# A planned order of steps with new durations, and the last modulation block summed in another stage

## The chip, the core and the metric

The kernel runs on one core of a Trainium2 chip, in one launch. Its time is device microseconds (us) from the runs; a profile of one execution stands beside it, and its span is from the first to the last instruction on the core.

Engines, by the names of the profile: PE is TensorE, DVE VectorE, ACT ScalarE, POOL GpSimd, SP the engine that issues most of the DMAs. Each of them runs its instructions in the order in which the program lists them. PSUM is the memory that TensorE writes, SBUF the on-chip working memory.

## The reference

One decoder layer on 1024 tokens of 1024 channels, in float32. A conditioning row `c` gives six modulation vectors, two sub-layers follow, each with a norm ahead and a norm behind:

```python
mod = silu(c) @ w_ada + b_ada
sh1, sc1, gt1, sh2, sc2, gt2 = split(mod, 6)

h = rms_norm(x, g_pre_mix) * (1 + sc1) + sh1
proj = h @ w_in                               # 512 columns u, 3 x 512 for the gated convolution
y_a = s5_mixer(u, ...)                        # state space groups, GELU, gated linear unit
y_b = short_conv_mixer(bg, cg, v, conv_w)
y = concat(head_rms_norm(y_a, g_out_ssm, 32), head_rms_norm(y_b, g_out_conv, 8))
x = x + gt1 * rms_norm(y @ w_out, g_post_mix)

h = rms_norm(x, g_pre_ffn) * (1 + sc2) + sh2
hid = causal_dwconv(h @ w_up, ffn_conv_w)     # 2 x 2816 columns
a, v = split(hid, 2)
x = x + gt2 * rms_norm((silu(a) * v) @ w_down, g_post_ffn)
```

`gt2` is the sixth vector, number 5 in the code, and it is used in the last line only.

## The kernel before

Matmuls of float32 precision are done as three matmuls of a rounded format: each operand is split into a high part (rounded on ScalarE) and the remainder (a subtraction on VectorE or GpSimd, line 381 or 867), and `mm3` (lines 475 to 479) adds high x high, high x low and low x high. Weights come as tiles of 128x1024 in three `raw` buffers, their splits in three `hl` buffers.

The stages, in order of time: the first norm and the projection of `u`; the tables of the state space part, small and large products on GpSimd and VectorE (sites `CL`, `WB`, `Pt`); the h tiles (`t_h`, lines 714 to 725) and the projection for the convolution; the state space part; the gated linear unit (`t_glu`, `t_gate`, the product `ya`); the statistics of the heads and their scaling (`t_head_out`: a matmul that spreads the factors, VectorE's product into `yb` or `ya`, ScalarE's rounding to `yh`, GpSimd's remainder `yl`); the output projection; two norms; the up projection; the down projection, which begins after 900 us; the last norm. Up and down projections use seven products in place of eight (Strassen's scheme), whose sums and differences are made on VectorE and GpSimd. In the up projection, `t_pair_weights` loads two weight tiles per pair (22 pairs, the first two apart), makes their differences and splits, `t_up` does the matmuls, `t_combine` the sums of products, `t_gate2` the convolution taps and the gate.

The modulation vectors are made without TensorE but for one tile: a tile of 128 rows of the transposed `w_ada` is multiplied with `cbc`, the row silu(c) spread over all partitions, and summed along the row into a column of `mod` (`ada_dot`: line 631 on VectorE, line 633 on GpSimd with ScalarE's sum). Vectors 0 and 1 are made at the start. `t_ada` loads the 32 tiles of vectors 2, 4, 3 and 5 in this order, into the buffers `WB`, `WBT` and `Pt`, once the tables that had them are used. `t_ada_dot` ends each vector with its bias and, but for number 3, a product with a norm's gain; number 5 goes to column group 3 of `col`. `t_colb` then writes that column to DRAM and loads it back over `cbc`, spread over the partitions; the last norm multiplies with it (`t_half`).

The order of the work is not written out by hand. Each task is a Python generator that yields a charge ahead of each step (an engine and a duration in us), an event to wait for, or a buffer to take. `Flow.run` simulates the engines with these charges when the program is built, and the instructions are emitted in the order in which it starts them: among the steps that can start on the engine that is next, that of the lowest priority number (`PRIO`) goes first. A step with a choice of engines (`T_`, `SITES`) goes to the one that would end it first. So the charges set no time on the chip, but they set the order on every engine and queue. The charges before are

```python
    def D_(n):
        return ("run", "dve", 0.07 + 1.04e-3 * n)

    def A_(n):
        return ("run", "act", 0.094 + 0.833e-3 * n)

    def G_(n):
        return ("run", "pool", 0.15 + 2.1e-3 * n)
```

for n elements in a row; the matmuls have charges of their own at each place. Steps of the up and down projection use a helper, `E_`, with 0.155 + 1.045e-3 n for VectorE.

Of the kernel before, what the change touches and what calls it, by code (L numbers as in the profile page):

```python
# [18 lines left out]
P = 128  # L19
# [182 lines left out]
class Flow:  # L202
# [85 lines left out]
    def run(self, until=None):  # L288

        while True:  # L290
            self._settle()
            if until is not None and until.t is not None:
                return
            ready = [th for th in self.threads if th[4][0] in ("run", "load", "pick")]
            if not ready:
                break
            plan = [(self._choice(th), th) for th in ready]
            t0, e = min((c[0], c[1]) for c, _ in plan)
            (start, e, cost), th = min(
                ((c, th) for c, th in plan if c[1] == e and c[0] <= t0 + 0.02), key=lambda p: p[1][:2]  # L300
            )
            end = self._pe_end(start, cost) if e == "pe" else start + cost
            self.free[e] = end
            if th[4][0] == "load":
                th[3] = start
                th[5] = end + LAND
            else:
                th[3] = end
            th[6] = e
            self._step(th, e if th[4][0] == "pick" else None)  # L310
        assert not self.threads, [(t[0], t[1], t[4], t[2].__name__, t[3]) for t in self.threads]
# [3 lines left out]
def hybrid_layer(ctx, tc, xT, w_adaT, w_ada0, w_u, w_bcv, w_out, w_up, w_down, glu_w, vec, ssm, con, out):  # L315
# [21 lines left out]
    def nm(s):  # L337
        uid[0] += 1
        return f"{s}_{uid[0]}"
# [19 lines left out]
    def load(dst, src):  # L359
        nc.sync.dma_start(dst, src)  # L360


    def D_(n):
        return ("run", "dve", 0.07 + 1.04e-3 * n)

    def A_(n):
        return ("run", "act", 0.094 + 0.833e-3 * n)

    def G_(n):
        return ("run", "pool", 0.15 + 2.1e-3 * n)  # L370

    def M_(n):
        return ("run", "pe", n)
# [363 lines left out]
    def t_u():  # L737
        yield ("wait", ev_X[0])
        yield ("get", "big", 3)
        yield ("get", "sm")  # L740
        up = [big() for _ in range(3)]
        uh = small()
        uo = [[t[:, :H], t[:, H:]] for t in up] + [[uh]]
        yield ("get", "k2")
        bs = k2("bs")[:2]
        for k in range(KD):
            yield ("wait", ev_X[k])
            w = wev["u", k // 2]
            yield ("wait", w[0])
            hl = w[1]  # L750
            for c4 in range(NT):
                n = len(uo[c4])
                o = (k % 2) * H + c4 * P
                if c4 == 0:
                    yield M_(0.215 * n)
                    for i in range(n):
                        pe.matmul(uo[0][i], hl[:, 0, o : o + P], X[k][0][i], start=k == 0, stop=False)
                    yield ("wait", ev_Xl[k])
                    yield M_(0.43 * n)
                    for i in range(n):  # L760
                        pe.matmul(uo[0][i], hl[:, 0, o : o + P], X[k][1][i], start=False, stop=False)
                    for i in range(n):
                        pe.matmul(uo[0][i], hl[:, 1, o : o + P], X[k][0][i], start=False, stop=k == KD - 1)
                else:
                    yield M_(0.6465 * n)
                    mm3(uo[c4], hl[:, 0, o : o + P], hl[:, 1, o : o + P], X[k][0][:n], X[k][1][:n], k == 0, k == KD - 1)
            fl.put("k2", 2)
            if k % 2:
                fl.spawn(t_bias(k // 2, hl, bs), PRIO["t_bias"])
        fl.fire(ev_u2)  # L770
        for c4 in (3, 0, 1, 2):
            fl.spawn(t_u_out(c4, uo[c4] + [None]), PRIO["t_u_out"])
        w = wev["u3",]
        yield ("wait", w[0])
        hl = w[1]
        yield ("get", "sm")
        uh2 = small()
        for k in range(KD):
            ks = slice(k * P, (k + 1) * P)
            yield M_(0.6465)  # L780
            mm3([uh2], hl[:, 0, ks], hl[:, 1, ks], X[k][0][1:], X[k][1][1:], k == 0, k == KD - 1)
            fl.put("k2", 2)
        fl.put("hl")
        fl.fire(ev_ups)
        ev_ups.tile = uh2
# [527 lines left out]
    def t_proj():  # L1313
        yield ("wait", ev_ups)

        for group in [bc_order[:PROJ_GROUP]] + [[t] for t in bc_order[PROJ_GROUP:]]:
            tiles_ = []
            for k in range(KD):
                ks = slice(k * P, (k + 1) * P)
                yield ("wait", ev_h[k])  # L1320
                for i, (n, c4) in enumerate(group):
                    if k == 0:
                        w = wev["p", n + c4]
                        yield ("wait", w[0])
                        yield ("get", "big")
                        tiles_.append((big(), w[1]))
                    o, hl = tiles_[i]
                    yield M_(1.293)
                    mm3([o[:, :H], o[:, H:]], hl[:, 0, ks], hl[:, 1, ks], hT[k][0], hT[k][1], k == 0, k == KD - 1)
            for (n, c4), (o, _) in zip(group, tiles_):  # L1330
                fl.put("hl")
                proj_ev[n + c4].tile = o
                fl.fire(proj_ev[n + c4])
        fl.put("k2", 4 * KD)
# [107 lines left out]
    def t_glu():  # L1442
        for s in range(NT):
            yield ("wait", sets[s]["z"])
        yield ("get", "sm")
        ev_stat["a"].tile = small()
        for c4 in range(NT):
            w = wev["g", c4 // 2]
            yield ("wait", w[0])
            gl = w[1]  # L1450
            yield ("get", "big")
            o = big()
            oo = [o[:, :H], o[:, H:]]
            for k in range(NT):
                ks = slice((c4 % 2) * H + k * P, (c4 % 2) * H + (k + 1) * P)
                yield M_(1.293)
                mm3(oo, gl[:, 0, ks], gl[:, 1, ks], zs[k][0], zs[k][1], k == 0, k == NT - 1)
            if c4 % 2:
                fl.put("hl")
            fl.spawn(t_gate(c4, o), PRIO["t_gate"])  # L1460
# [24 lines left out]
    def t_ada():  # L1485

        yield ("wait", ev_v[NT - 1])
        for m in (2, 4, 3, 5):
            for k in range(KD):
                tag = ("WB", "WBT", "Pt")[k % 3]  # L1490
                yield ("get", tag)
                w = table(tag, [1024])
                yield L_(512)
                load(w, w_adaT[m * D + k * P : m * D + (k + 1) * P, :])
                fl.spawn(t_ada_dot(m, k, w, tag), PRIO["t_ada_dot"])
# [42 lines left out]
    def t_out():  # L1538
        for bi, (hf, lo, hi) in enumerate(blocks):
            n = hi - lo  # L1540
            outs, og4 = {}, {}
            so = [[], [Event() for _ in range(NT)]]
            for part, dp in w_seq[bi]:
                w = wev["o", bi - ((part, dp) in (kept(bi - 1) if bi else [])), part, dp]
                yield ("wait", w[0])
                hl = w[1]
                if part == first:
                    yield ("get", "big")
                    outs[dp] = big((P, 2, H))
                for k4_ in range(NT):  # L1550
                    k = k4_ + (0 if part == "A" else NT)
                    yield ("wait", ev_y[k][hf])
                    yield M_(1.293 * n / H)
                    for d2 in range(2):
                        ks = slice(k4_ * 256 + d2 * P, k4_ * 256 + (d2 + 1) * P)
                        mm3(
                            [outs[dp][:, d2, :n]], hl[:, 0, ks], hl[:, 1, ks], [yT[k][0][hf][:, lo:hi]], [yT[k][1][hf][:, lo:hi]],
                            part == first and k4_ == 0, part == last and k4_ == NT - 1,
                        )
                if (part, dp) not in kept(bi):  # L1560
                    fl.put("hl")
                if part == last:
                    og4[dp] = Event()
                    fl.spawn(t_out_evac(bi, n, dp, outs[dp], og4, so, len(og4) - 1), PRIO["t_out_evac"])
            if hi == H:
                fl.put("k2", 4 * KD // 2)
            fl.spawn(t_resid(bi, og4, so), PRIO["t_resid"])
        fl.fire(ev_out)
# [811 lines left out]
    def t_put(tag):  # L2380
        yield ("land",)
        fl.put(tag)

    def t_colb():

        yield ("wait", ev_mod[5])
# [24 lines left out]
        fl.spawn(t_combine(i), PRIO["t_combine"])  # L2411
    g_threads()
    w_threads()
    fl.spawn(t_colb(), PRIO["t_ada_dot"])
    for tb in range(NTB):
        fl.spawn(t_evict(tb), PRIO["t_evict"])
# [81 lines left out]
```

## Time and profile before

| | |
|---|---|
| time, median of three runs | 1140.34 us (1136.54 to 1142.83) |
| profiled execution | 1135.78 us, of it a span of 1134.0 us |
| TensorE busy | 1049.4 us, 93% of the span, 5012 matmuls |
| VectorE busy | 889.3 us, 78% |
| ScalarE busy | 482.9 us, 43% |
| GpSimd busy | 473.9 us, 42% |
| mean granted TensorE clock | 0.969 |
| HBM traffic | 151 GB/s over the span |

A matmul's end is modelled in the profile, so a busy TensorE is not one at its peak. Busy shares are means over stages with different limits; the table of stages, which gives the busy time of each engine in stretches of time, tells them apart. A row of the waits names the waiting engine, its buffer and line, what it waited for, and the us in total, the times and the longest.

### The profile page before, as it was taken

How to read it: one execution, taken by the hardware profiler on the slowest of the kernel's cores; microseconds unless marked ns; L12 is line 12 of the kernel's file. 1: busy time of each engine (PE TensorE's matmuls, PEld its weight loads, DVE VectorE, ACT ScalarE, POOL GpSimd, SP SyncE). 2: the span in 40 equal slices, each digit the busy share in tenths (PEclk: the TensorE clock that was granted, in tenths of full speed). 3: DMA queues.
4: the chain of work that ended last, by engine and by line, in shares of the span. 5: the costliest groups of instructions: out<-in, count | busy, mean ns of one | idle time of the engine just before them, and what ended most of it. 6: DMA issues, size and time to landing. Idle time of an engine off the chain costs nothing. (4 is left out here: it accounts for less than half of the span.)

```text
span 1134.0 us, 13972 instructions
## 1 busy us (share of the span) xinstructions
PE 1049.4 (93%) x5012; PEld 848.6 (75%) x5012; DVE 889.3 (78%) x1218; ACT 482.9 (43%) x672; POOL 473.9 (42%) x469
## 2 busy tenths in 40 slices
PE   2988889999897998898999999999999999999996
PEld 2756677778554898687778888888888887888885
DVE  6769779777998288989888799788888887554763
ACT  4435412322344456565433333333334455454552
POOL 4799445671486134212343444343443220342002
PEclk9979889999898998999999999999999999999999
DMA  7633313236754356423552233223323597999337
GB/s 276 233 132 131 113 38 98 79 121 213 254 197 133 126 176 196 158 75 121 186 167 96 72 123 128 79 90 112 112 91 104 207 262 245 261 220 293 117 93 139
DMA packets 88821, 172.07 MB, mean 152 GB/s; under 512 B 8752, under 2 KB 34096, under 8 KB 88752
## 3 DMA queue, kind: packets, MB, share of 16 engines
q1 hardware_dynamic: 80688, 156.50, 41.0%
q0 software_dynamic: 8064, 14.68, 7.8%
q8 instruction: 39, 0.64, 0.2%
q14 instruction: 30, 0.25, 0.1%
HBM read 133.69 MB, written 37.46 MB: 151 GB/s over the span
## 5 line engine op out<-in xcount | busy, mean ns | idle before, releaser
L381 POOL TENSOR_TENSOR hl<-w,hl 128x1024 fp32r<-128x1024 f32 x40 | 102.9, 2575 | 284.7 <-ACT hl L1882 149.0
L381 POOL TENSOR_TENSOR w<-w,w 128x512 f32<-128x512 f32 x57 | 84.2, 1477 | 81.9 <-DVE hl L867 78.9
L1882 ACT CAST hl<-w 128x1024 fp32r<-128x1024 f32 (+1 forms) x65 | 66.5, 1023 | 47.7 <-issue 22.9
L2210 POOL DMA_DIRECT2D wd<-in_w_down_dram x44 | 38.5, 884 | 113.0 <-DMA wd<-in_w_down_dram 45.4
L867 DVE TENSOR_TENSOR wl<-wd,wh 128x512 fp32r<-128x512 f32 x77 | 50.9, 686 | 38.5 <-ACT wh L2214 38.2
L477 PE MATMUL big<-yl,hl 128*128 128x256 f32 (+1 forms) x192 | 63.4, 330 | 7.5 <-POOL yl L381 7.5
L2214 ACT CAST wh<-wd 128x512 fp32r<-128x512 f32 x77 | 46.1, 619 | 53.2 <-DMA wd<-in_w_down_dram 51.3
L870 DVE SCALAR_TENSOR_TENSOR ca<-big,vec,ca 128x896 f32<-128x896 f32 (+1 forms) x92 | 65.2, 740 | 3.2 <-ACT ca L2048 3.1
L475 PE MATMUL big<-h,hl 128*128 128x512 f32 x192 | 63.4, 412 | 3.3 <-ACT h L723 1.5
L867 DVE TENSOR_TENSOR hl<-w,hl 128x1024 fp32r<-128x1024 f32 (+1 forms) x45 | 52.9, 1174 | 16.4 <-ACT hl L1882 16.3
L461 ACT CAST hl<-w 128x1024 fp32r<-128x1024 f32 x43 | 44.9, 1044 | 48.0 <-PE big L479 31.2
L475 PE MATMUL big<-yh,hl 128*128 128x256 f32 (+1 forms) x192 | 64.9, 338 | 0.1
L477 PE MATMUL big<-h,hl 128*128 128x512 f32 x192 | 61.4, 401 | 3.0 <-DVE h L725 3.0
L479 PE MATMUL big<-h,hl 128*128 128x512 f32 x192 | 61.1, 400 | 2.8 <-POOL hl L381 2.8
L479 PE MATMUL big<-yh,hl 128*128 128x256 f32 (+1 forms) x192 | 63.3, 330 | 0.1
L475 PE MATMUL big<-s,hl 128*128 128x512 f32 x160 | 63.2, 395 | 0.0
L477 PE MATMUL big<-s,hl 128*128 128x512 f32 x160 | 63.0, 394 | 0.0
L479 PE MATMUL big<-s,hl 128*128 128x512 f32 x160 | 62.8, 393 | 0.0
L475 PE MATMUL big<-h2h,hl 128*128 128x512 f32 (+1 forms) x160 | 60.2, 376 | 0.0
L870 DVE SCALAR_TENSOR_TENSOR cv<-big,vec,cv 128x896 f32<-128x896 f32 (+1 forms) x84 | 58.5, 740 | 1.3 <-ACT cv L2048 1.3
L477 PE MATMUL big<-h2l,hl 128*128 128x512 f32 (+1 forms) x160 | 59.4, 372 | 0.0
L479 PE MATMUL big<-h2h,hl 128*128 128x512 f32 (+1 forms) x160 | 59.4, 372 | 0.0
(361 smaller groups left out, 3162.2 us busy)
## 6 DMA issues: line engine op xcount, KB each, us to landing
w<-in_w_up_dram SPq DMA_DIRECT2D x44, 512.0 KB, 4.0
w<-g_dr SPq DMA_DIRECT2D x35, 512.0 KB, 6.1
g_dr<-cv SPq DMA_DIRECT2D x53, 256.0 KB, 2.2
wd<-in_w_down_dram SPq DMA_DIRECT2D x44, 256.0 KB, 7.7
wd<-in_w_down_dram POOLq DMA_DIRECT2D x44, 256.0 KB, 6.5
w<-in_w_out_dram SPq DMA_DIRECT2D x20, 512.0 KB, 3.6
WBT<-in_w_adaT_dram SPq DMA_DIRECT2D x16, 512.0 KB, 4.6
w<-in_w_bcv_dram SPq DMA_DIRECT2D x13, 512.0 KB, 3.8
```

What stands on the lines that cost most here:

```text
L381: {"dve": dve, "pool": pool}[e].tensor_tensor(o, a, b, op)
L461: act.copy(t[:, 0, :], w)
L475: pe.matmul(outs[i], wh, xh[i], start=start, stop=False)
L477: pe.matmul(outs[i], wh, xl[i], start=False, stop=False)
L479: pe.matmul(outs[i], wl, xh[i], start=False, stop=stop)
L867: (eng or dve).tensor_tensor(o, a, b, op)
L870: dve.scalar_tensor_tensor(o, a, s, b, op0, op1)
L1882: act.copy(t[:, 0, :n], w)
L2210: pool.dma_start(w, block_of(made[1], kk), accum_op=ADD)
L2214: act.copy(hi, w)
```

## The change

Two things. The planner's charges are made longer: VectorE 0.155 + 1.045e-3 n, ScalarE 0.19 + 0.84e-3 n, GpSimd 0.18 + 2.2e-3 n, six matmuls of 512 columns 1.362 in place of 1.293, and a VectorE step that starts while GpSimd is planned busy costs a quarter more. And vector 5 leaves `t_ada`; a new task, `t_ada_last`, loads its eight tiles into `raw` buffers in the up projection, the k-th when the loads of weight pair 4 + k are issued, multiplies and sums them on VectorE, and adds the bias and the gain at the end.

```diff
@@ Flow.run
+            if e == "dve" and self.free.get("pool", 0.0) > start:
+                cost *= 1.25
             end = self._pe_end(start, cost) if e == "pe" else start + cost
...
     def D_(n):
-        return ("run", "dve", 0.07 + 1.04e-3 * n)
+        return ("run", "dve", 0.155 + 1.045e-3 * n)
     def A_(n):
-        return ("run", "act", 0.094 + 0.833e-3 * n)
+        return ("run", "act", 0.19 + 0.84e-3 * n)
     def G_(n):
-        return ("run", "pool", 0.15 + 2.1e-3 * n)
+        return ("run", "pool", 0.18 + 2.2e-3 * n)
...
-                    yield M_(0.6465 * n)
+                    yield M_(0.681 * n)
...
-                    yield M_(1.293)
+                    yield M_(1.362)
...
@@ t_ada
-        for m in (2, 4, 3, 5):
+        for m in (2, 4, 3):
...
+    def t_ada_last():
+        for k in range(KD):
+            yield ("wait", pw[4 + k]["loaded"])
+            yield ("get", "raw")
+            w = wp.tile([P, 1024], F32, tag="raw", name=nm("w"))
+            yield L_(512)
+            load(w, w_adaT[5 * D + k * P : 5 * D + (k + 1) * P, :])
+            yield ("land",)
+            yield ("run", "dve", 1.23)
+            dve.scalar_tensor_tensor(w, w, 1.0, cbc, MUL, MUL, accum_out=mod[:, 5, k : k + 1])
+            fl.put("raw")
+        yield ("run", "dve", 0.15)
+        ada_bias(5, 0, KD)
+        yield ("run", "dve", 0.15)
+        tt(col[:, 3, :], mod[:, 5, :], vt[:, slice(*_VC["g_post_ffn"])], MUL)
+        fl.fire(ev_mod[5])
...
+    fl.spawn(t_ada_last(), PRIO["t_sums"])
     fl.spawn(t_colb(), PRIO["t_ada_dot"])
```

The same new matmul charge stands in the gated linear unit and, by columns, in the output projection. The product's own charge in `ada_dot`, 1.19 on VectorE, stays.

More of the change, by code (lines that the diff above doesn't have):

```diff
@@ L779, in t_u @@
             ks = slice(k * P, (k + 1) * P)
-            yield M_(0.6465)
+            yield M_(0.681)
             mm3([uh2], hl[:, 0, ks], hl[:, 1, ks], X[k][0][1:], X[k][1][1:], k == 0, k == KD - 1)
@@ L1455, in t_glu @@
                 ks = slice((c4 % 2) * H + k * P, (c4 % 2) * H + (k + 1) * P)
-                yield M_(1.293)
+                yield M_(1.362)
                 mm3(oo, gl[:, 0, ks], gl[:, 1, ks], zs[k][0], zs[k][1], k == 0, k == NT - 1)
@@ L1552, in t_out @@
                     yield ("wait", ev_y[k][hf])
-                    yield M_(1.293 * n / H)
+                    yield M_(1.362 * n / H)
                     for d2 in range(2):
```

## The prediction, made before the changed kernel was run

> **What bounds the kernel now.** I read the table of stages first, then the waits of the stage that the moved work leaves, then that stage's engines in order of time, and last the stage that the work goes to. In the table each row has a stretch, its length, the busy time of TensorE, its weight loads, VectorE, ScalarE and GpSimd, then the granted clock, the DMA share and the GB/s.
>
> ```profile
> core 0: us, PE busy (x) PEld busy (x) DVE busy (x) ACT busy (x) POOL busy (x), PEclk, DMA share, GB/s
> 100.00:120.00 20.00, 12.81 (x45) 9.44 (x44) 20.00 (x15) 8.48 (x12) 20.00 (x13) 0.85 0.66 210
> 330.00:340.00 10.00, 8.48 (x31) 4.09 (x29) 10.00 (x12) 3.47 (x5) 10.00 (x5) 1.00 0.67 233
> 340.00:350.00 10.00, 3.37 (x9) 1.92 (x10) 10.00 (x8) 2.10 (x4) 9.49 (x5) 0.63 0.64 213
> 350.00:360.00 10.00, 10.00 (x38) 6.26 (x36) 8.48 (x16) 4.72 (x6) 0.13 (x1) 0.86 0.10 11
> 360.00:380.00 20.00, 20.00 (x84) 15.04 (x85) 9.09 (x10) 10.58 (x16) 11.82 (x8) 1.00 0.59 205
> 560.00:900.00 340.00, 339.31 (x1489) 277.44 (x1487) 288.20 (x335) 131.91 (x145) 139.97 (x86) 1.00 0.33 110
> ```
>
> The up projection (last row) is TensorE's: idle for 0.7 of 340 us, at full clock. Between 330 and 350 us, where the heads are scaled ahead of the output projection, it is not: VectorE is full, GpSimd nearly, TensorE is idle for 1.52 + 6.63 = 8.15 us, and its clock is low during the idle stretch and after it. From 360 us on TensorE is full again, so what is won before that is kept. Between 100 and 120 us both elementwise engines are full as well, and TensorE is idle for 7.19 us.
>
> The waits between 327 and 352 us (in total, times, longest) name the late work:
>
> ```profile
> ACT yh L1431 <- DVE yb L870: 10.1, 4, 4.9
> PEld big L477 <- POOL yl L381: 8.2, 2, 6.8
> PE big L477 <- POOL yl L381: 7.5, 2, 6.5
> ```
>
> TensorE waits for GpSimd's remainder of a head (yl), ScalarE's rounding before it waits for VectorE's scaling (yb). VectorE's instructions in order of time show what stands ahead of yb:
>
> ```profile
> 334.01 2.75 DVE L631 SCALAR_TENSOR_TENSOR Pt<-Pt,cbc 128x1024 f32<-128x1024 f32 x1
> 336.69 0.08 DVE L631 DVE_READ_ACCUMULATOR Pt<-Pt,cbc 128x1 f32 x1
> 336.69 2.27 DVE L631 SCALAR_TENSOR_TENSOR WB<-WB,cbc 128x1024 f32<-128x1024 f32 x1
> 338.89 0.08 DVE L631 DVE_READ_ACCUMULATOR WB<-WB,cbc 128x1 f32 x1
> 338.89 0.74 DVE L870 SCALAR_TENSOR_TENSOR yb<-yb,vec,sm 128x512 f32<-128x512 f32 x1
> 339.55 1.10 DVE L381 TENSOR_TENSOR ya<-zh,zl 128x512 f32<-128x512 f32 x1
> 340.57 2.28 DVE L631 SCALAR_TENSOR_TENSOR WBT<-WBT,cbc 128x1024 f32<-128x1024 f32 x1
> 342.79 0.08 DVE L631 DVE_READ_ACCUMULATOR WBT<-WBT,cbc 128x1 f32 x1
> 342.79 0.73 DVE L870 SCALAR_TENSOR_TENSOR yb<-yb,vec,sm 128x512 f32<-128x512 f32 x1
> ```
>
> L631 is the product with the conditioning row. The block's fourth group, number 5, is the last eight of them, and all eight lie here; three stand ahead of the yb at 342.79, for which TensorE stalls. GpSimd in the same stretch, and two rows of it from elsewhere as its durations beside less VectorE work:
>
> ```profile
> 327.69 4.65 POOL L381 TENSOR_TENSOR yl<-yb,yh 128x512 fp32r<-128x512 f32 x2
> 332.30 3.37 POOL L381 TENSOR_TENSOR hl<-w,hl 128x1024 fp32r<-128x1024 f32 x1
> 335.64 2.24 POOL L381 TENSOR_TENSOR yl<-yb,yh 128x512 fp32r<-128x512 f32 x1
> 337.84 2.26 POOL L381 TENSOR_TENSOR ya<-zh,zl 128x512 f32<-128x512 f32 x1
> 340.06 1.72 POOL L381 TENSOR_TENSOR yl<-yb,yh 128x512 fp32r<-128x512 f32 x1
> 341.74 3.32 POOL L381 TENSOR_TENSOR hl<-w,hl 128x1024 fp32r<-128x1024 f32 x1
> 345.03 4.47 POOL L381 TENSOR_TENSOR yl<-yb,yh 128x512 fp32r<-128x512 f32 x2
> ```
>
> ```profile
> 359.87 11.95 POOL L381 TENSOR_TENSOR yl<-ya,yh 128x512 fp32r<-128x512 f32 x8 [10.38 <-ACT yh L1431]
> ```
>
> ```profile
> 645.11 2.40 POOL L381 TENSOR_TENSOR hl<-w,hl 128x1024 fp32r<-128x1024 f32 x1 [7.03 <-ACT hl L1882]
> ```
>
> **The change part by part. Part A, eight products leave the stage before the output projection.** Their VectorE time there, all eight with their accumulator reads:
>
> ```profile
> 327.60:352.00 24.40, 15.78 (x16) 0.81 0.63 216
> ```
>
> VectorE gives up 15.78 us of 24.4. The yb at 342.79 has 2.75 + 2.27 + 2.28 = 7.3 us of them directly ahead. But GpSimd has no pause from 327.69 to 345.03, so it is late next. Its six rows up to there sum to 17.56 us; at 11.95 / 8 = 1.49 for the five ops of 512 and 2.40 for the two of 1024 they would be 12.25, a stretch of 5.3. Seven VectorE ops with two SBUF inputs ran beside them, five of them products of group 5. Lower end, GpSimd's order kept: 5.3 x 5/7 = 3.8 us. Upper end, the stall gone with its clock: 8.15 idle, plus 3.37 x 0.37 = 1.25 and 10 x 0.14 = 1.4 of low clock, 10.8. The middle, 7.3, is also what VectorE's side gives, and VectorE is free to take one of the two weight splits (hl, 3.3 us) off GpSimd. I take **-7.3**. Their eight loads (512 KB each) leave SP's queue too, where the weights of the output projection stand between them; the DMA share was 0.64 to 0.67, so I cost that at nothing.
>
> A rule speaks for a larger gain. The Trainium skill, SBUF — State Buffer, section "Who interferes with whom", says that a VectorE instruction with two SBUF inputs and a GpSimd instruction that reads SBUF exclude each other, the second waiting for the first to end. By it five products of 1.2 us ahead of the late yl hold GpSimd for 6.0 us, and the lower end would be 6.0 in place of 3.8. The trace agrees in kind: 2.28 us for a product beside a GpSimd op, against 1.21 for the shortest one below.
>
> **Part B, the same eight come back in the up projection**, one to a pair of weight tiles, from pair 4 to 11, on VectorE alone, with three small adds at the end. The product's durations (shortest, median, longest) in one of its three buffers, and a VectorE op of 512 that meets GpSimd in the up projection (0.69 where it doesn't, in a row further down):
>
> ```profile
> L631 DVE SCALAR_TENSOR_TENSOR WBT<-WBT,cbc x14: 1210/1226/3307, 39.0 to 350.5; 128x1024 f32<-128x1024 f32 x14
> ```
>
> ```profile
> L867 DVE TENSOR_TENSOR wf<-w,wf 128x512 fp32r<-128x512 f32 x17 | 23.9, 1407 | 17.0 <-ACT wf L1882 15.8
> ```
>
> VectorE is idle for 340 - 288.2 = 51.8 us there, 3.05 for each of the 17 pairs. A product of 1.21 to 1.97 (15.78 / 8) fits; one of 3.31 doesn't, by 0.3 us. What is queued behind it: the combine and the convolution taps, which free TensorE's PSUM tiles. Ends: 0 and, with a whole split of 2.40 waited for each time, 1.21 + 2.40 - 3.05 = 0.56 by eight, 4.5 us. Nearest is the mean of 1.97, which is hidden; for orders in which it falls ahead of a combine I take **+1**.
>
> The load takes the third raw buffer and a place in SP's queue behind each pair's weights. Two rows for the cover, SP's weight issues of the next pair and ScalarE's first split of it:
>
> ```profile
> 667.89 10.12 SPq L360 DMA_DIRECT2D w<-in_w_up_dram  x2
> ```
>
> ```profile
> 682.51 1.05 ACT L1882 CAST hl<-w 128x1024 fp32r<-128x1024 f32 x1
> ```
>
> The first of the two tiles is issued 14.6 us ahead of its split, the second at about 677.7, once GpSimd has freed its buffer. A product frees its buffer some 6 us after its load is issued (landing and 1.2 to 2 us), so I cost the buffer at nothing; with the cover gone each pair would be late by up to those 6 us. The two transfers that spread the summed column (a store and a reload of the row) move with it, to the middle of the up projection; their user comes after 900 us.
>
> **Part C, the order of everything is planned anew.** Old and new charge stand against these rows:
>
> ```profile
> L867 DVE TENSOR_TENSOR wl<-wd,wh 128x512 fp32r<-128x512 f32 x77 | 50.9, 686 | 38.5 <-ACT wh L2214 38.2
> L477 PE MATMUL big<-yl,hl 128*128 128x256 f32 (+1 forms) x192 | 63.4, 330 | 7.5 <-POOL yl L381 7.5
> L2214 ACT CAST wh<-wd 128x512 fp32r<-128x512 f32 x77 | 46.1, 619 | 53.2 <-DMA wd<-in_w_down_dram 51.3
> ```
>
> For 512 elements VectorE was charged 0.602 and is now charged 0.690 (row: 0.686), ScalarE 0.520 and 0.620 (row: 0.619), GpSimd 1.225 and 1.306 (1.49 above). The old plan slipped low-priority products into gaps of VectorE that weren't there; the two products between 334.01 and 338.89, planned at 1.19 each, took 5.0. The new plan sees fewer such gaps, and adds a quarter where GpSimd is busy. No row shows the new order, so I bound it by the other stage where both engines are full. The operations of h, 30 in all between 60 and 125 us, and one at its stretched size:
>
> ```profile
> L725 DVE SCALAR_TENSOR_TENSOR h<-x,mod,h 128x512 fp32r<-128x512 f32 x15 | 19.5, 1335 | 0.0
> L714 DVE SCALAR_TENSOR_TENSOR x<-x,col,rb 128x512 f32<-128x512 f32 x8 | 8.4, 1070 | 0.0
> L381 DVE TENSOR_TENSOR x<-x,rb 128x512 f32<-128x512 f32 x7 | 7.9, 1138 | 0.0
> ```
>
> ```profile
> 114.43 1.57 DVE L714 SCALAR_TENSOR_TENSOR x<-x,col,rb 128x512 f32<-128x512 f32 x1
> ```
>
> They sum to 35.8 us; alone, at 0.74 (the yb rows), they are 22.2. Best: TensorE's idle time of 100 to 120 us goes, 7.19 and 12.81 x 0.15 = 1.9 of clock, 9.1 us. Worst: all 30 beside a GpSimd op, 47.1, so 11.3 more, with clock in proportion 14.3. The charges move towards the rows, so a gain is nearer than a loss, but priorities are as before and 0.86 is still far from 1.57: I take a third of the best, **-3**.
>
> **The sum.** -7.3 + 1 - 3 = -9.3. The profiled execution took 1135.78 us, so 1126.5. It was 4.6 us below the median of the three runs (1140.34); against that median, 1131.0, 0.8% less. A change under 0.5%, 5.7 us, can't be told from none here.
>
> **The rivals.** *GpSimd stays the bound and the order brings nothing*: -3.8 + 1 = -2.8, 1137.5. For it: GpSimd without a pause up to the late yl. Against it: six of its rows are stretched by what is removed.
>
> *The product blocks and is blocked in the up projection*: 4.5 in place of 1, -5.8, 1134.5. For it: wf at 1.41 against 0.69; against it: 3.05 us free in each pair. The lock of part A, from the Trainium skill's SBUF — State Buffer, section "Who interferes with whom", is a rule for this one as well.
>
> *Slower: the new order puts more of the table building on GpSimd beside the operations of h.* It is first in time, at 60 to 125 us, and TensorE waits for h. Price: part C's worst, +14.3, gives -7.3 + 1 + 14.3 = +8.0, 1148.3. The 13.6 us of stretch at 0.83 for each op say that some 16 of the 30 meet a GpSimd op now. One more costs 0.83, with clock 1.05, so six more use up the 6.3 that the other parts give, and eleven or twelve more make it slower by 0.5%. For it: a VectorE that looks longer sends more pieces to GpSimd. Against it: most of those tables are GpSimd's already.
>
> **How the numbers follow.** Forecast 0.60, GpSimd bound 0.16, blocked product 0.08, slower 0.16. Faster than 1134.6: 0.58 of the first, 0.01 of the second, 0.02 of the third, 0.61. Slower: 0.14 of the last. Same: 0.25. Low end: -10.8 - 9.1 is -19.9, 1120. High end: the slower rival's middle, +4, 1144; what lies above it is half of that rival, and the low tail little. The likeliest case alone: 1122 to 1135.
>
> **What would show it.** Right: no L631 product after the third group's between 320 and 352 us, TensorE's wait for yl there under 2 us, the output projection's full stretch starting 5 to 10 us sooner relative to the stage before; eight products between 600 and 800 us of 1.2 to 2.4 us with TensorE's idle time in the up projection still near 1 us. Part C shows in the start of the output projection as a whole: the time at which the conv projection ends, earlier or later. Wrong: TensorE's idle time between 60 and 130 us grown, GpSimd waits for yl as before, or a gap in the up projection each time a product runs.

## The result, and the profile after

The changed kernel took 1205.92 us (1201.1 to 1207.36) against 1139.59 us for the kernel before on the same chip: a ratio of 1.0578 [1.0547, 1.0608], 66 us slower. The prediction was 1131, with a range up to 1144. The profiled execution took 1207.36 us (span 1205.6), the granted clock fell from 0.969 to 0.937. TensorE has the same 5012 matmuls, busy for 1059.7 us in place of 1049.4. So of the 71.6 us between the two spans 61 are TensorE standing still, and 10 are the same matmuls taking longer, at the lower clock.

Where TensorE stands, the longest waits of the changed kernel (engine, buffer and line, what it waited for, then us in total, times, longest; lines are three higher than before):

```profile
PE sm L1087 <- POOL Bd L1079: 38.4, 1, 38.4
PE big L760 <- ACT X L683: 15.1, 3, 8.3
PE big L2260 <- ACT hl L1885: 14.1, 1, 14.1
PE sm L482 <- DVE hm L870: 7.9, 4, 3.8
...
PE sm L2126 <- ACT sn L2021: 6.0, 1, 6.0
...
PE big L480 <- POOL yl L384: 0.8, 1, 0.8
```

The last row is part A's stall, 7.5 us before. The first row alone is over half of the loss. The third is the start of the down projection, the fourth and fifth lie in the up projection; the second was there before.

The table of stages after, with the columns of before:

```profile
60.00:80.00 20.00, 16.83 (x74) 13.70 (x74) 14.24 (x34) 4.38 (x10) 19.27 (x47) 0.79 0.26 88
80.00:100.00 20.00, 2.62 (x14) 1.82 (x13) 19.47 (x28) 10.55 (x17) 19.99 (x34) 0.63 0.07 24
100.00:120.00 20.00, 0.00 (x0) 0.00 (x0) 13.24 (x12) 4.79 (x8) 19.92 (x19) 0.50 0.00 0
120.00:140.00 20.00, 18.84 (x107) 13.98 (x108) 14.57 (x22) 13.89 (x15) 5.95 (x5) 0.84 0.54 180
...
560.00:900.00 340.00, 323.62 (x1396) 261.43 (x1397) 277.58 (x346) 128.50 (x155) 134.24 (x80) 0.97 0.41 123
...
1000.00:1020.00 20.00, 10.07 (x36) 8.03 (x37) 11.19 (x14) 7.81 (x10) 0.00 (x0) 0.66 0.67 218
```

From 82 to 121 us TensorE does nothing, and no DMA moves from 100 to 120. In the up projection it is idle for 16.4 of the 340 us from 560 to 900, where it was 0.7; over the whole stage, which begins later now, for 19.4 of 417 us in place of 2.4 of 391.

To compare kernels I read from the trace when TensorE begins its first matmul on h (conv projection), zh (gated linear unit), yh (output projection), s (the sums of h2, so the up projection) and wh (down projection). All in us. The row of before is that of the runs beside after; each ratio is against the runs of before beside it (medians 1139 to 1143):

| kernel | h | zh | yh | s | wh | s to wh | median | ratio [95%] |
|---|---|---|---|---|---|---|---|---|
| before | 96 | 295 | 330 | 520 | 910 | 391 | 1139.6 | |
| after | 135 | 334 | 370 | 551 | 968 | 417 | 1205.9 | 1.0578 [1.0547, 1.0608] |
| e1, move alone | 97 | 293 | 329 | 513 | 910 | 397 | 1137.9 | 0.9981 [0.9949, 1.0013] |
| e2, charges alone | 135 | 330 | 365 | 548 | 959 | 412 | 1198.0 | 1.0497 [1.0453, 1.0540] |
| e3, after, taps held | 135 | 333 | 369 | 547 | 963 | 416 | 1203.7 | 1.0548 [1.0507, 1.0588] |
| e4, charges, taps held | 135 | 330 | 366 | 547 | 959 | 412 | 1197.4 | 1.0488 [1.0448, 1.0528] |
| e5, matmul charges | 131 | 326 | 361 | 541 | 930 | 389 | 1151.6 | 1.0083 [1.0046, 1.0119] |
| e6, after, small steps 0.30 | 98 | 315 | 348 | 525 | 946 | 421 | 1181.7 | 1.0343 [1.0300, 1.0387] |
| e7, elementwise charges | 102 | 308 | 342 | 517 | 920 | 403 | 1159.2 | 1.0156 [1.0118, 1.0195] |
| e8, the quarter alone | 104 | 312 | 341 | 519 | 910 | 391 | 1150.2 | 1.0080 [1.0054, 1.0106] |
| e9, charges late only | 95 | 296 | 330 | 507 | 910 | 403 | 1147.2 | 1.0075 [1.0044, 1.0105] |
| e10, charges early only | 136 | 331 | 366 | 544 | 941 | 397 | 1168.5 | 1.0258 [1.0226, 1.0290] |
| e11, group 5 behind heads | 96 | 296 | 334 | 521 | 912 | 391 | 1136.5 | 0.9970 [0.9950, 0.9990] |
| e12, same, matmul charges late | 97 | 295 | 336 | 536 | 923 | 388 | 1145.4 | 1.0056 [1.0030, 1.0083] |
| e13, after, sums first | 135 | 330 | 365 | 545 | 976 | 431 | 1207.1 | 1.0582 [1.0555, 1.0608] |
| e14, after, shift columns first | 119 | 316 | 348 | 529 | 948 | 419 | 1183.7 | 1.0388 [1.0341, 1.0435] |
| e15, after, both repairs | 100 | 324 | 369 | 549 | 962 | 413 | 1200.4 | 1.0524 [1.0504, 1.0544] |
| e16, both and sums first | 99 | 323 | 367 | 547 | 980 | 432 | 1208.5 | 1.0593 [1.0571, 1.0615] |
| e17, move, no products | 98 | 297 | 332 | 514 | 907 | 393 | 1134.6 | 0.9962 [0.9936, 0.9989] |
| e18, move, no loads either | 95 | 296 | 334 | 514 | 907 | 393 | 1136.0 | 0.9959 [0.9939, 0.9980] |

By these marks 39.2 us are lost at zh (38.7 already at h), 7.5 won back by s, 26.3 lost in the up projection and 12.8 behind it (the last matmul begins 228 us after wh in place of 215): 39.2 - 7.5 + 26.3 + 12.8 = 70.8 in the two profiled executions, whose spans differ by 71.6.

**The first place: h.** The table that TensorE waits for is no later than before. GpSimd's small copies into Bd, after and then before:

```profile
119.31 0.55 POOL L1079 COPY Bd<-ssm 64x64 f32<-64x64 f32 x1
```

```profile
120.46 0.31 POOL L1076 COPY Bd<-ssm 64x64 f32<-64x64 f32 x1
```

What differs is what stands behind it. TensorE runs its matmuls in the order listed. Before, the table's first matmuls (the taps, L1084) came behind 72 matmuls on h; now they come ahead of all 576. TensorE's matmuls on h and on Bd, their durations (shortest, median, longest), then first and last start, after and then before:

```profile
L478 PE MATMUL big<-h,hl x192: 389/389/793, 134.9 to 322.8; 128*128 128x512 f32 x192
L1087 PE MATMUL sm<-ssm,Bd x64: 182/183/236, 121.0 to 290.5; 128*32 128x16 f32 x64
```

```profile
L475 PE MATMUL big<-h,hl x192: 387/389/793, 96.2 to 293.1; 128*128 128x512 f32 x192
L1084 PE MATMUL sm<-ssm,Bd x64: 182/183/205, 126.4 to 247.2; 128*32 128x16 f32 x64
```

So h stands behind Bd, though its first tile is there at about 84 us (first row of the next fence). Between Bd at 121 and h at 135 come 14 us of other work: bias matmuls and the last matmuls on X, which the old order had done by 96 us, and transposes of WB, which it put behind the first matmuls on h. The Trainium skill, TensorE: Matmul & The Clock Gate, section "The mechanism", says that matmuls start and end in program order, without reordering; the trace agrees, with this wait of 38.4 us.

Two more things are late at the same time. On VectorE the last shift column (shl), which a bias matmul needs, stood ahead of the h operations; now it stands behind them, and an h ahead of it waits for a buffer that GpSimd's table work holds (WB at line 384):

```profile
83.50 0.75 DVE L728 SCALAR_TENSOR_TENSOR h<-x,mod,h 128x512 fp32r<-128x512 f32 x1
...
113.15 1.57 DVE L728 SCALAR_TENSOR_TENSOR h<-x,mod,h 128x512 fp32r<-128x512 f32 x1 [3.42 <-POOL WB L384]
114.64 1.04 DVE L698 TENSOR_TENSOR shl<-mod,shl 128x1 fp32r<-128x1 f32 x1
```

Before, it was done at 76:

```profile
76.14 0.25 DVE L695 TENSOR_TENSOR shl<-mod,shl 128x1 fp32r<-128x1 f32 x1
```

And SP's queue stops at a store of K, the taps that TensorE makes and ScalarE copies out, with the conv weights behind it:

```profile
78.00 0.38 SPq L363 DMA_DIRECT2D Tr<-in_con_dram  x1
123.84 0.33 SPq L363 DMA_DIRECT2D k_dr<-K  x1
```

```profile
SPq L363 <- ACT K L1093: 45.4, 1, 45.4
```

That store alone does not make the weights late. In e3 below it does not stand ahead of them, and they wait 48.0 us for VectorE's split of an earlier tile, which frees their buffer; they are issued at 126.2 us, in the changed kernel at 130.8.

### The profile page after: what moved, and what is told of

Its sections match the earlier page's. It is cut to its first block, busy times and chain, and to the rows that moved or that the text cites. A ratio compares the mean times of both kernels' runs of the same rounds, so it can differ in the third digit from the quotient of the medians.

```text
span 1205.6 us, 13931 instructions
## 1 busy us (share of the span) xinstructions
PE 1059.7 (88%) x5012; PEld 854.4 (71%) x5012; DVE 870.7 (72%) x1226; ACT 480.0 (40%) x670; POOL 449.8 (37%) x462
## 5 line engine op out<-in xcount | busy, mean ns | idle before, releaser
L384 POOL TENSOR_TENSOR hl<-w,hl 128x1024 fp32r<-128x1024 f32 x38 | 95.1, 2505 | 327.6 <-ACT hl L464 167.6
L478 PE MATMUL big<-h,hl 128*128 128x512 f32 x192 | 62.5, 407 | 6.2 <-DVE z L873 5.8
L2260 PE MATMUL big<-wh,hl 128*128 128x512 f32 x130 | 51.2, 394 | 14.1 <-ACT hl L1885 14.1
L480 PE MATMUL big<-h,hl 128*128 128x512 f32 x192 | 60.5, 397 | 0.0
```

The source lines that it names most:

```text
L384: {"dve": dve, "pool": pool}[e].tensor_tensor(o, a, b, op)
L478: pe.matmul(outs[i], wh, xh[i], start=start, stop=False)
L480: pe.matmul(outs[i], wh, xl[i], start=False, stop=False)
L2260: pe.matmul(o, gh, wh, start=kk == 0, stop=False)
```

## The experiments

**Move or charges.** e1 has the old charges and the new place of group 5, e2 the new charges and the old place.

```diff
 # e1: the two hunks of t_ada and t_ada_last, charges as before
 # e2: the hunks of Flow.run, D_, A_, G_ and M_, t_ada as before
```

> The old charges, with group 5's eight products moved to the up projection. Theory 1 (the loss is the new charges', the move is sound): the stall of the yl wait before the output projection goes, the up projection stays at under 3 us of idle TensorE, 1128 to 1136 us against 1140. Theory 2 (the moved products and their raw buffer cost the time): the up projection loses some 25 us as in the changed kernel, 1155 to 1170 us.

> The new charges, with group 5 left in its old place. Theory 1: nearly the whole loss is here, 1195 to 1215 us, with the 38 us wait of TensorE for GpSimd's Bd between 80 and 121 us. Theory 2: about 1165 to 1180 us, the stall of 38 us alone, with an up projection as short as before.

The move alone makes no difference that can be told (ratio 0.998); the charges alone cost 5.0% of the 5.8%, 57 us. On top of them the move costs some 9 us more (1.0578 against 1.0497). The longest waits of e2 are the changed kernel's:

```profile
PE sm L1086 <- POOL Bd L1078: 39.8, 2, 38.7
...
PE big L2259 <- ACT hl L1884: 11.5, 1, 11.5
```

In e1, part A shows as predicted and is taken back later. Its table of stages:

```profile
330.00:340.00 10.00, 8.20 (x32) 3.78 (x30) 9.41 (x10) 4.64 (x6) 4.74 (x4) 1.00 0.24 71
340.00:350.00 10.00, 9.80 (x42) 6.79 (x38) 6.62 (x11) 5.25 (x7) 2.21 (x3) 1.00 0.85 298
...
513.00:910.00 397.00, 390.44 (x1702) 317.81 (x1702) 345.25 (x411) 158.15 (x186) 168.54 (x99) 0.99 0.41 133
```

TensorE is idle for 2.0 us between 330 and 350 in place of 8.15, and the output projection ends at 452 in place of 459. The up projection begins 7 us sooner and ends at the same 910. Its row in the kernel before, idle for 2.4 us where e1 has 6.6:

```profile
520.00:910.00 390.00, 387.60 (x1699) 316.70 (x1698) 332.40 (x389) 156.62 (x183) 157.15 (x98) 1.00 0.36 121
```

**Holding the taps.** If the taps alone are the cause, it helps to make them wait for the projection.

```diff
+            if s == 0:
+                yield ("wait", proj_ev[5])
             yield ("get", "sm")
             kp = small()[:, :P]
```

> The changed kernel, with the planner holding the first taps matmul until the first two tiles of the conv projection are planned. Theory 1a (TensorE's order alone makes the 38 us wait): the wait goes and the time falls by 35 to 45 us, to 1160 to 1172. Rival 1b (GpSimd's tables are the pole of the first 330 us anyway, so the wait turns up later, at the first use of the tables): under 15 us gained, 1190 or more.

> The new charges with group 5 in its old place and the first taps matmul held in the same way. Theory 1 and 1a: 1155 to 1175 us, within 10 us of the changed kernel with the same hold, since the move is worth little. Theory 2: clearly under that kernel, by 20 us or more, near 1140.

Nothing gained: 1203.7 and 1197.4, h at 135 as before the edit. In e3 the next late thing takes the wait:

```profile
PE sm L804 <- DVE shl L698: 33.5, 1, 33.5
```

The waits end at 115.7 us for shl, at 121.0 for Bd in the changed kernel, and in e3 TensorE then stands another 5.0 us for WB, to 123.5. So the stall has several releasers stacked within 8 us of each other, and the one that the waits name is only the last.

**Which charge.** e5 has only the matmul charges, e7 only those of VectorE, ScalarE and GpSimd, e8 only the quarter, all with group 5 in its old place. e6 is the changed kernel with the small preparation steps ahead of the tables, nearly all of them GpSimd's, charged nearer to what they take (line 897 in the changed kernel: most of them 0.21 to 0.88 us, for 16 to 128 elements). The copies into Bd are not among them; these four steps and two memsets have a charge of 1.8 of their own and take 2.5 us.

```diff
-    def queued(site, cost=0.21):
+    def queued(site, cost=0.3):       # e6
```

> Only the matmuls' new charges (5% longer in the early stages); all else as before. Its VectorE order has the last shift column behind the first h operations, as the changed kernel has. Theory 3 (the early loss is one flip in the order, shift columns behind h, whatever charge flips it): the gated linear unit begins 30 to 42 us later than before's 295 us, and the time is 1165 to 1185 us. Theory 4 (the longer VectorE charges make it): within 6 us of before, 1134 to 1146.

> The changed kernel with one number changed, GpSimd's small preparation steps charged 0.30 in place of 0.21 (0.2 to 1.1 in the traces); its VectorE order has the shift columns ahead of h again. Theory 3: the gated linear unit begins near 295 us again and the time falls to 1155 to 1175 us, the rest being the loss of the up and down projections. Theory 4: 1190 or more, as with the taps held.

> Only the new charges of VectorE, ScalarE and GpSimd, without the quarter more beside GpSimd and without the matmuls' charges. Theory 3: early stages as before (295 us). If these charges make the loss of the up projection and at the start of the down projection, 1155 to 1170 us; if the quarter does, 1134 to 1146 us.

> Only the quarter more for a VectorE step that starts while GpSimd is planned busy. Theory 3: early stages as before. If the quarter makes the loss of the up projection and at the start of the down projection, 1155 to 1175 us; if the plain charges do, 1134 to 1146 us.

Each single charge costs 0.8 to 1.6%, 9 to 18 us; the three add to 36, all at once cost 57. They stop at different rows. In e5 h is 35 us late for another table (WB), and its stages behind the conv projection are 12 us shorter than before; in e6 h is on time, but TensorE then stands in the middle of the conv projection:

```profile
PE big L1126 <- DVE WB L381: 28.3, 2, 23.9
```

```profile
PE big L1129 <- POOL WB L384: 21.7, 2, 13.5
...
PE sm L1087 <- POOL Bd L1079: 10.0, 4, 4.4
```

Every one of these orders puts matmuls of the tables in front of conv matmuls while GpSimd is still at the tables; the old order did so least. Ahead of the first taps stand 72 matmuls on h before, 24 in e8, 6 in e6 and e7, none in e5. No single charge is the cause, and the theory of one flip (shift columns behind h) missed: with it e5 lost less than forecast, and without it e6 still reaches zh 20 us late.

**Early or late.** A flag is set when the plan of the conv projection ends; e9 uses the new charges only from there on, e10 only up to there, both with the move. They are not exact halves of the change: on their side of the flag they lengthen every matmul charge made by `M_` by 5%, also those that the change leaves alone (in e9 those of the up and down projection, 0.43 and 0.687; in e10 those of the tables).

```diff
+PH = [False]                          # set at the end of t_proj
-        return ("run", "dve", 0.07 + 1.04e-3 * n)
+        return ("run", "dve", 0.155 + 1.045e-3 * n if PH[0] else 0.07 + 1.04e-3 * n)   # e9; e10: not PH[0]
```

> The whole change, but the new charges hold only from the end of the conv projection's plan on; ahead of it the order of the kernel before is kept. Theory, several late things each with its own place: the table stage is on time again (end of the conv projection at 293 us as in the move alone, not 334), and the losses in the up projection and at the start of the down projection stay: 1205.9 - 41 = 1165, so the later losses are 27 us of the whole. Rival, the later losses only follow from the late start: they go too, and the time is that of the move alone, 1138 to 1145.

> The counterpart: the whole change with the new charges up to the end of the conv projection's plan and the old ones from there. Theory, each place on its own: the early loss alone, 1138 + 41 = 1179, the up projection at 397 us as in the move alone and no wait of 10 us or more for hl at the start of the down projection. Rival, the late start brings on the later losses: 1200 to 1206.

Neither theory holds whole. Over the move alone (differences of the ratios times 1140) the early charges cost 32 us and the late ones 11, but together 68. The early loss is 38 us at zh in e10, of which 8 are won back by the end; its up projection is that of the move, 397, in spite of the late start. So a late start does not by itself make the later stages slower. What is missing in the sum, some 25 us, is found only in the changed kernel, where the later order was planned with the new charges from a changed early order: 417 us in the up projection against 403 and 397. By the marks of the profiled executions, where 34 us are missing, 12 lie ahead of s, 15 in the up projection and 7 behind it. Since e9 and e10 also lengthen charges that the change does not, this sum shows that something is missing, not how much of it comes from the two halves meeting. In e9 the start of the down projection is left, and a wait in the up projection (second row), with VectorE's instructions ahead of the first:

```profile
PE big L2264 <- ACT hl L1889: 9.6, 1, 9.6
PE sm L2130 <- ACT sn L2025: 7.2, 1, 7.2
```

```profile
921.89 6.70 DVE L873 TENSOR_TENSOR wl<-wd,wh 128x512 fp32r<-128x512 f32 x11
928.51 0.68 DVE L873 TENSOR_TENSOR cv<-cv,gs 128x512 f32<-128x512 f32 x1
...
940.46 1.22 DVE L873 TENSOR_TENSOR cv<-cv,ca 128x1024 f32<-128x1024 f32 x1 [0.58 <-ACT ca L2074]
```

Eleven remainders of down weights (wl) stand in one block ahead of the subtraction that frees the buffer of the last pair; its gate comes at 940.46, at 931.75 before. Between the pair's last combine and that gate stand 22 remainders, 8 before.

```profile
930.49 1.28 DVE L867 TENSOR_TENSOR wl<-wd,wh 128x512 fp32r<-128x512 f32 x2
931.75 1.23 DVE L867 TENSOR_TENSOR cv<-cv,ca 128x1024 f32<-128x1024 f32 x1
```

**The last gate.** e13 is the changed kernel with the sums of the gates (`t_sums`) ahead of the remainders.

```diff
-                fl.spawn(t_sums(i // 2, even, r["b"]), PRIO["t_sums"])
+                fl.spawn(t_sums(i // 2, even, r["b"]), 12)
```

> The changed kernel with one number altered: the five-fold sums of a pair of gates (the subtractions that free a gate's buffer and the stores behind them) get priority 12 in place of 14, ahead of the remainders of the down projection's weights, which have 13. Between the last pair's combine and its gate VectorE then has 10 remainders in place of 25 (8 in the kernel before). Theory, the start of the down projection is late because the last gate stands behind remainders that nobody waits for: TensorE's wait of 14.1 us for hl goes to under 3, and 11 to 14 us of the 66 come back, about 1193. Rival, the stores and reloads on SP's queue are late anyhow, or the remainders that were in front are then late in their turn: 1200 to 1206.

The local reading was right and the gain zero. The wait for hl is gone, the down projection is 11 us shorter (217 against 228), and the up projection 14 longer (431 against 417), with a wait for weights (wf) that was 1.8 us:

```profile
PE sm L482 <- DVE wf L870: 15.8, 6, 3.1
...
PE big L2260 <- ACT hl L1885: 1.5, 1, 1.5
```

**Repairing the start.** e14 plans the shift columns before h; e15 does so too and moves the tables' matmuls behind h.

```diff
-    "t_sh": 9,
+    "t_sh": 3,                        # e14, e15, e16
-    def queued(site, cost=0.21):
+    def queued(site, cost=0.4):       # e15, e16
+        for s_ in range(NT):          # e15, e16, ahead of t_out
+            yield ("wait", sets[s_]["z"])
```

> The changed kernel with the shift columns at priority 3 in place of 9, so that VectorE's last shl stands ahead of the first h, with no h waiting for a GpSimd table. The table matmuls (taps and the transposes of WB) still stand ahead of every conv matmul on TensorE. Theory, three stacked late things: TensorE stands until Bd is there at about 121, but nothing else is late behind it, so h begins at 122 in place of 135: 1190 to 1196. Rival, the shift columns alone are the cause: h begins near 97 and the early loss of 39 us goes, 1167.

> As the run with the shift columns first, and GpSimd's small steps charged 0.40 in place of 0.21, so that the tables look later and their matmuls stand behind the first 66 (taps) and 96 (transposes) conv matmuls on TensorE, as in the kernel before (72 and 96); the output projection is planned once all state sets are done. Theory: h begins at 97 to 100, the conv projection ends at 295 to 305 in place of 334, and 30 to 39 us come back: 1167 to 1176. Rival, the two engines, not the order, are the bound of this stage under the new charges: h on time but short of tables later, conv projection's end at 315 or more, 1185 or more, as in the run with 0.30.

> Both repairs of the early stage and the sums at priority 12, in the changed kernel. Theory, separate places: the two gains add, 1167 to 1176 less 11 to 14, so 1153 to 1165, and what is left over the move alone (1138) is the up projection's 13 to 20 us. Rival, the places are not separate, each repair moves the loss elsewhere: above 1170.

With the shift columns first 22 us come back, more than the 10 to 16 expected: GpSimd's table is done 9 us sooner too (the first tap matmul at 112), and TensorE stands 3.6 us for it there; over the whole run its waits for Bd are 11.6 us. With both repairs h begins at 100, as theory had it, and the conv matmuls end at 284, 10 us sooner than in the kernel before; but the stage ends at 324. TensorE's waits between 280 and 330 us:

```profile
PE sm L1424 <- DVE hl L873: 10.0, 1, 10.0
PE big L1261 <- DVE St L384: 4.3, 1, 4.3
PE big L1261 <- DVE St L873: 4.3, 1, 4.3
```

The state matmuls (L1261), which need tables, are now last, and a head's factor matmul (L1424) stands ahead of them and waits for VectorE. The rival of e15 came true: with h first again, the stage still ends 29 us later than in the kernel before (zh at 324, 295 before). e16 adds nothing (1208.5): its third repair makes the down projection 10 us shorter and the up projection 20 longer, much as in e13 (11 and 14).

**Where the move's gain went.** e11 keeps group 5 in `t_ada`, old charges, but lets it wait for the last head; e12 adds the matmul charges behind the conv projection.

```diff
+            if m == 5:
+                yield ("wait", ev_y[KD - 1][1])
             for k in range(KD):
```

> The kernel before, old charges, with group 5 left in its block but loaded and summed only once the last head is scaled, so during the output projection, where VectorE is idle for about half of 360 to 400 us. Theory, the move alone gained nothing because its eight products and its transfers take back in the up projection what the output projection won: here the output projection starts and ends 6 to 7 us sooner and the up projection stays at 390 us: about 1133, ratio 0.994. Rival, what is won ahead of the output projection is lost at any later place, since something else sets the start of the up projection: 1138 to 1140, ratio 0.998 to 1.000.

> As the run with the fourth group behind the heads, with the new matmul charges (5% longer) from the end of the conv projection's plan on. In the run with the matmul charges alone the stages behind the conv projection took 818 us against 830. Theory, those 12 us are the better order's: 1133 - 12 = 1121, ratio about 0.983. Rival, they came from the 35 us late start, in which loads ran ahead: 1133, ratio 0.994, or no better than before.

e11 missed: the up projection is 391 us, but the gated linear unit's stage takes 38 us in place of 35, so the output projection starts no sooner; 0.997 is less than can be told from no change by the 0.5% set above. In e12 the 12 us of e5 don't come; it is 6 us slower than before. That they came with e5's late start is the reading that is left, but not shown: e12, like e9, also lengthens matmul charges that e5 leaves alone.

e17 and e18 are the move alone with the same order of steps, without the products, and without products and loads. Both leave out the sum of the sixth vector (its bias is still added).

```diff
-            dve.scalar_tensor_tensor(w, w, 1.0, cbc, MUL, MUL, accum_out=mod[:, 5, k : k + 1])   # e17, e18
-            load(w, w_adaT[5 * D + k * P : 5 * D + (k + 1) * P, :])                              # e18
```

> The move alone (old charges), with the order of steps unchanged, but without the eight products of group 5 themselves: their tiles are loaded and read by nobody, the sum is zero (so this part of the output's scale is left out); the two transfers that spread the sum stay. In the move alone the up projection took 397 us against 390. Theory, the products on VectorE block the combine and the taps: the up projection takes 390 to 391 and 6 us come back, 1132, ratio 0.993. Rival A, the eight loads and the third raw buffer (costed at nothing) are the price: still 397, 1138, ratio 0.998. Rival B, it is only the order around them: 397 here and without the loads.

> As the run without the products, and without their eight loads of 512 KB as well, order unchanged (the same part of the output's scale is left out). Theory, products are the price: the same time as without the products, 1132, the up projection at 390 to 391. Rival A, the loads are: here 390 and 1132, there 397 and 1138. Rival B, the order around them is: 397 and 1138 in both.

The up projection takes 393 us in both, against 397 with the products and 391 before. The table of stages of e17 over the stretch shown for e1, with 4.8 us idle where e1 has 6.6 (3.8 in its own stage, 514.0 to 907.4):

```profile
513.00:910.00 397.00, 392.24 (x1712) 318.93 (x1713) 336.51 (x399) 159.95 (x190) 163.47 (x101) 1.00 0.41 135
```

So of the 6 us the products cost 4, the loads under 1, and 2 are the order planned around them. The medians of e1, e17 and e18 lie too close (their intervals overlap); this rests on the profiled executions, one of each.

## Why the prediction was wrong

**Part A was right for the move alone, and had no part in the changed kernel.** -7.3 was predicted; in e1 TensorE's wait for yl at 330 to 350 is gone, VectorE has taken both weight splits (hl) off GpSimd, and the output projection ends 7 us sooner. About 2 of these are won ahead of zh: from zh to the last yh matmul it is 4.6 us less in e1, 8.6 in e17, 5.6 in e18. The lower end of 3.8 is under all three. The 6.0 by the rule of the Trainium skill, SBUF — State Buffer, section "Who interferes with whom", lies amid them, so these runs do not tell which of the two is nearer. (The 3.8 is a little high: beside the seven two-input operations counted, an eighth, on ya and St, begins at 343.45 us, and 5.3 x 5/8 is 3.3.)

In the changed kernel the wait for yl is 0.8 us, but in e2, which leaves group 5 in its old place, it is the same:

```profile
PE big L479 <- POOL yl L383: 0.8, 1, 0.8
```

There the late start gave VectorE the time: the last product of group 5 starts at 352.7 us, 12 us ahead of the output projection, where in the kernel before it started 20 us behind its begin. So under the new charges the move had nothing left to win here.

**Part B was sized wrong.** +1 was taken; it is +6 in the move alone. The two edges stood at 0 and 4.5: the products' 4 us are inside, near the upper one, and the 2 us of order around them were in no term. The loads were rightly costed at nothing; the raw buffer, held until its product has run, was not tried apart from the product.

**Part C is the step that failed.** -3 was taken between -9.1 and +14.3; it is +57 (charges alone). The bound came from the durations of the h operations beside GpSimd, and these went the way that was forecast. From 60 to 125 us in the changed kernel:

```profile
L728 DVE SCALAR_TENSOR_TENSOR h<-x,mod,h 128x512 fp32r<-128x512 f32 x14 | 14.6, 1067 | 6.8 <-POOL WB L384 3.4 <-POOL CL L384 3.3
L384 DVE TENSOR_TENSOR x<-x,rb 128x512 f32<-128x512 f32 x7 | 7.4, 1061 | 0.0
L717 DVE SCALAR_TENSOR_TENSOR x<-x,col,rb 128x512 f32<-128x512 f32 x8 | 7.3, 918 | 0.0
```

They sum to 29.3 us for 29, where 30 took 35.8: shorter by a few us, as part C hoped, while TensorE stood for 38. The prediction priced an order by how long its instructions take. What an order costs is what it puts in front of what on an engine that cannot pass a waiting instruction, and that has no bound in any duration: the matmuls on h waited because table matmuls (the sixteen-column taps, and with them the transposes of WB and the bias matmuls with shl) were listed first. That this is part of the cause e14 shows, where planning the shift columns earlier moves h from 135 to 119 us and brings 22 us back; that it is not all of it e15 shows, where h is on time and the stage is late all the same. The slower rival named the right stretch (60 to 125 us, tables on GpSimd, TensorE waiting for h) with the wrong mechanism, the stretched operations, and so with a price of 14.3 in place of 39. Its condition did not come either: GpSimd is busy for 61.7 us between 60 and 125 us, 61.8 before.

"The charges move towards the rows, so a gain is nearer than a loss" was the argument for the sign. Each charge did move towards its row, and each alone lost 9 to 18 us. The steps whose charges stayed (GpSimd's small steps, planned at 0.21) were then probably the ones planned too early against the rest; but giving them 0.30 or 0.40 moved the wait instead of ending it. That the old order was better than any of these neighbours is what the runs show; they do not show why, beyond the waits of each.

The two signs set down for this were both seen: TensorE's idle time between 60 and 130 us grown, and the conv projection's end later. The range was too narrow because it was made from one stage's durations, though the whole program's order was planned anew.

Left open: the 25 us that neither the early nor the late charges show alone, and why the stage ends late in e15. The up projection's 417 us have visible waits (hm 7.9, sn 6.0 and 2.6, wf 1.8) and come with another order than e9's, but which of its steps decides was not tried. None of the versions beats the kernel before by more than the 0.5% that can be told.

## What to carry to other kernels

When an edit makes a planner order the whole program anew, do not price it from durations: the loss depends on how long a late producer can hold up everything listed behind its consumer. Ask for each in-order engine and queue which instruction of the critical stage would stand behind which late one, and keep the stages that are already good in their old order (in e9 that left 11 of 68 us). A wait that the profile names is the last of several: lifting it is worth the distance to the next one, and repairs in one place can come back as a wait elsewhere.

## What was not expected of the hardware

SP's queue issued nothing for 45.4 us behind one small store, since that store waited for a result of the same stalled TensorE; what this cost is less than it looks, as e3's 48.0 us show. And a stall of TensorE costs again when it ends, in the granted clock: it is 0.50 from 100 to 120 us, still 0.56 from 121 to 127 us, where a bias matmul of 512 columns takes 0.63 us, and 1.00 from 127 to 140 us, where it takes 0.40.
